# Residual loads behind the projection weights, an earlier norm order, an own constant semaphore, and a last norm without GpSimd, in an encoder block on eight cores

## The chip, the cores and the metric

The kernel runs on the 8 cores of one Trainium2 chip, two dies of four cores each. Every core computes half of one of four sequences (2048 tokens) and no core waits for another. The metric is the time on the device of the slowest core, in microseconds (us).

An execution is sometimes in a slow state: the cores of one die are granted a lower TensorE clock, and the time is longer, by 4 to 19% in the clear cases. One of the changed kernel had mean granted clocks of 0.859 to 0.862 on one die and 0.984 to 0.988 on the other, and took 1184.42 us where the fast ones took 1040.13 and 1041.25; the longest (`poke_end`) took 1240.4 instead of 1040.59.

Several chips appear. The result and the profiles of before and after come from one, called the first chip below.

## The reference, cut to what matters

```python
u = rms_norm(h, g_mix)                        # h: tokens x 1024
z = u @ w_in                                  # value, gate, pool input, two gates: 5 x 1024 columns
y_conv = conformer_conv(z[..., :c1], z[..., c1:c2], ...)   # GLU, depthwise conv, LayerNorm, swish, matmul
y_pool = multi_scale_pool(z[..., c2:c3], ...)
merged = gate_a * y_conv + gate_b * y_pool
h = h + merged @ w_o                          # output projection and residual
v = rms_norm(h, g_ffn)
h = h + (silu(v @ w_ffn_gate) * (v @ w_ffn_up)) @ w_ffn_down
return rms_norm(h, g_final)                   # the last norm
```

## The kernel before: the parts that matter

The program has a list of instructions for each engine, with waits on semaphores where data cross engines. Channels lie on the partitions and tokens along the free dimension, so the sum of squares of a norm goes through a matmul with a matrix of 1/1024, then Ln and Exp(-0.5 x) on ScalarE (ACT), and VectorE (DVE) multiplies.

The start: x comes in six pieces. Each is squared, summed and normed while TensorE (PE) already multiplies earlier pieces ("tiles" are PE work).

```python
    x_load(0)
    for (o, i_) in ((pc[:], pc_d.ap()), (invc[:], ic_d.ap()), (emask[:], em_d.ap())):
        S.dma(SP, cst, o, i_, val=48)         # three constants, ONE semaphore, all three awaited
    for p in range(NX):
        if p:
            x_load(p)                         # on the GpSimd (POOL) queue
        if p < 4:
            load_one()                        # two weight pieces, same queue
            load_one()
    ...
    s1_squares(4)                             # squares on ScalarE, sums on GpSimd
    tiles((0, 1, 2), (6,))
    s1_norm(3)
    tiles((0, 1, 2), (7,))
    tiles((3,), range(4))
    s1_squares(5)
    s1_norm(4)
    tiles((3,), range(4, KC))
    tiles((4,), range(1))
    s1_norm(5)
    ...
```

The output projection: eight weight pieces `wo0` to `wo7` come through a ring of nine slots on the GpSimd queue; the residual (x again, 4 blocks of 2 MB) comes on the SyncE (SP) queue.

```python
    for b in range(NB):
        C(6, b)
    release("co6")                            # frees the slot into which wo7 is loaded
    def x_res(b):
        S.dma(SP, h1_sem[b], h1b[b][:]..., xr_d.ap()[b])
    for b in (0, 1, 3):
        x_res(b)                              # SyncE is free: issued early
    for b in range(NB):
        C(7, b)
    release("co7")
    x_res(2)
```

The end: for the last 256 tokens, GpSimd does three of the eight multiplies of the last norm. ScalarE has multiplied those three tiles by the gain earlier, and writes 1/rms to SBUF for GpSimd.

```python
        for c in (4, 0, 5, 1, 6, 2, 3, 7) if last else range(KC):
            x = h[:, c, o:o + w_]
            if last and c in (4, 5, 6):
                tt(POOL, x, x, rs, ALU.mult)
            else:
                stt(DVE, x, x, pcc(PC_GFIN, c), psum[7][:, 0:w_], ALU.mult, ALU.mult)
        # ... then four stores of two tiles each on SyncE, and a wait for them
```

## Time and profile before

| | before |
|---|---|
| time, median (fast runs) | 1057.15 us |
| span of the slowest core (core 4) | 1052.6 us |
| PE busy | 1002.3 us (95%) |
| PE waits for the last projection weight | 4.3 us (2.1 to 5.0 on the eight cores) |
| last matmul weight load to the end of the program, core 4 | 13.7 us |

PE is busy nearly always. A change can only win where PE waits, where its clock is lowered, and at the two ends, where PE has nothing to do.

From the page of the kernel before: the busy time of each engine (PEld is PE's weight load), and the chain that ended last by engine.

```profile
PE 1002.3 (95%) x5630; PEld 489.4 (46%) x5696; DVE 449.3 (43%) x690; ACT 309.3 (29%) x504; POOL 158.5 (15%) x184
PE 86%; DMA 4%; DVE 4%; ACT 4%; issue 2%; POOL 0%; SPq 0%; ACTq 0%; POOLq 0%; DVEq 0%
```

The instructions at the line that closes the program block, kernel before, core 4 (durations in ns, then the times of the first and last start in us). A small "q" marks the engine's own sequencer.

```profile
L973 POOLq EVENT_SEMAPHORE  x2: 17/17/17, 1052.4 to 1052.5; - x2
L973 POOLq DRAIN  x1: 11366/11366/11366, 1041.0 to 1041.0; - x1
L973 SPq DRAIN  x1: 7/7/7, 1045.9 to 1045.9; - x1
```

SyncE's DRAIN comes after its wait for the last store, so all results were in memory at 1045.9 us. The program still ran until 1052.5, because GpSimd's DRAIN took 11.37 us, the first 2 us of them beside its three multiplies. It ended 9.3 us after the last of these. The chain of waits does not show this: it ends at a GpSimd multiply at 1042.3 us, and the last ten microseconds have no row.

The waits of the PE in the output projection (us in all, number, longest), and the loads there with their microseconds from issue to landing (kernel before, core 4):

```profile
PE ps L352 <- DMA wslot_60<-w_o: 4.3, 1, 4.3
```

```profile
h1b_216<-xr SPq DMA_DIRECT2D x1, 2048.0 KB, 11.4
h1b_217<-xr SPq DMA_DIRECT2D x1, 2048.0 KB, 20.5
h1b_219<-xr SPq DMA_DIRECT2D x1, 2048.0 KB, 27.0
...
wslot_61<-w_o POOLq DMA_DIRECT2D x1, 256.0 KB, 3.5
wslot_63<-w_o POOLq DMA_DIRECT2D x1, 256.0 KB, 14.8
wslot_68<-w_o POOLq DMA_DIRECT2D x1, 256.0 KB, 21.7
wslot_60<-w_o POOLq DMA_DIRECT2D x1, 256.0 KB, 23.5
```

The four weight pieces are alike. The first was issued at 490.9 us, before the residual loads of 494 us, and took 3.5 us. The others came after them and took 15 to 23.5 us; PE reached the last one 4.3 us too early.

The start: VectorE's instructions that read a piece of x, in order of time (start, us; busy, us; instruction; idle time before it and what ended that), kernel before, core 4.

```profile
13.00 2.42 DVE L373 SCALAR_TENSOR_TENSOR uT<-xb_177,pc_s,ps 128x160 bf16<-128x160 f32 x8 [3.20 <-DMA emask_s<-emask]
15.43 1.23 DVE L366 TENSOR_TENSOR sqx<-xb_178 128x1024 f32<-128x1024 f32 x1
21.92 3.22 DVE L373 SCALAR_TENSOR_TENSOR uT<-xb_178,pc_s,ps 128x256 bf16<-128x256 f32 x8 [2.61 <-ACT ps L363]
...
50.03 4.56 DVE L373 SCALAR_TENSOR_TENSOR uT<-xb_180,pc_s,ps 128x416 bf16<-128x416 f32 x8 [7.44 <-ACT ps L363]
65.55 4.82 DVE L373 SCALAR_TENSOR_TENSOR uT<-xb_181,pc_s,ps 128x448 bf16<-128x448 f32 x8 [10.96 <-ACT ps L363]
```

The rows with `uT` are the norms of pieces 0, 1, 3 and 4; the row with `sqx` squares piece 1. The first norm waits for a constant that it doesn't read (`emask`), and VectorE is idle for 7.4 and 11 us before the norms of pieces 3 and 4, waiting for ScalarE. PE pays for the latter: one of its rows at that place is

```profile
67.56 0.35 PE L352 MATMUL ps<-uT,wslot_60 128*128 128x448 bf16 x1 [0.24 <-DVE uT L373]
```

that is, matmul by matmul at the pace of VectorE.

### The profile page before, as it was taken

To read this page: it belongs to the slowest core of one execution; us is meant where nothing else is said; L and a number is where in the kernel's file an instruction comes from. 1 tells how busy PE (TensorE), PEld (TensorE's weight loads), DVE (VectorE), ACT (ScalarE), POOL (GpSimd) and SP (SyncE) were. 2 spreads that over 40 slices of the span, in tenths; PEclk is the share of its full clock that TensorE was granted. 3 is DMA by queue.
4 is the path that set the end of the run, shared out by engine and by line. 5 is a ranking of instruction groups with operands and counts; after the bars stand their busy time and mean duration, and the time that the engine had idled before them with its cause. 6 is when DMAs were issued, how large, how long until landed. Compare 5 with 4: busy or idle time off the path is not lost.

```text
span 1052.6 us, 15608 instructions; the slowest of 8 cores (1042.4 to 1052.6 us)
## 1 busy us (share of the span) xinstructions
PE 1002.3 (95%) x5630; PEld 489.4 (46%) x5696; DVE 449.3 (43%) x690; ACT 309.3 (29%) x504; POOL 158.5 (15%) x184
## 2 busy tenths in 40 slices
PE   3899999999989999999899999999999999999994
PEld 1645555555434444444344444444444444444483
DVE  4442879974279533233536521221211211343453
ACT  2643233344487611221134311111111111121121
POOL 2233022221420000000347001111000000000000
PEclk9989999999999999999999999999999999999998
DMA  9605887667253111112946445554222103312112
GB/s 219 204 0 81 167 165 160 138 160 148 59 89 61 32 31 31 31 30 59 295 177 149 102 77 95 96 92 72 41 40 34 19 1 126 115 81 81 80 81 80
DMA packets 34251, 99.90 MB, mean 95 GB/s; under 512 B 3968, under 2 KB 7168, under 8 KB 31616
## 3 DMA queue, kind: packets, MB, share of 16 engines
q0 software_dynamic: 17744, 43.00, 22.9%
q1 hardware_dynamic: 16432, 55.90, 18.3%
q8 instruction: 47, 0.77, 0.3%
q14 instruction: 28, 0.23, 0.1%
HBM read 111.93 MB, written 21.04 MB: 126 GB/s over the span
## 4 chain that ended last, share of the span: by engine, by line
PE 86%; DMA 4%; DVE 4%; ACT 4%; issue 2%; POOL 0%; SPq 0%; ACTq 0%; POOLq 0%; DVEq 0%
PE ps L352 80%; PE ps L627 5%; DMA wslot_60<-w_o 2%; DVE uT L373 1%; DMA emask_s<-emask 1%; DVE sqx L366 1%; ACT L363 1%; DMA wslot_68<-w_pool_out 1%; ACT sqx L363 0%; ACT ps L363 0%; POOL h2b_259 L366 0%; ACT zt_206 L363 0%; DVE d_2_108 L366 0%; DVE d_2_104 L366 0%; DVE d_2_100 L366 0%
## 5 line engine op out<-in xcount | busy, mean ns | idle before, releaser
L352 PE MATMUL ps<-uT,wslot_60 128*128 128x512 bf16 (+6 forms) x223 | 53.5, 360 | 9.1 <-DVE uT L373 8.3
L352 PE MATMUL ps<-mT,weff 128*128 128x512 bf16 x249 | 60.0, 385 | 0.4
L352 PE MATMUL ps<-uT,wslot_65 128*128 128x512 bf16 (+6 forms) x213 | 45.1, 357 | 0.3 <-issue 0.2
L363 ACT ACTIVATE sgf_225<-ps 128x512 f32<-128x512 f32 x30 | 17.9, 597 | 81.3 <-PE ps L352 77.6
L363 ACT ACTIVATE sgf_226<-ps 128x512 f32<-128x512 f32 x29 | 17.3, 597 | 82.3 <-PE ps L352 82.3
L352 PE MATMUL ps<-uT,wslot_61 128*128 128x416 bf16 (+6 forms) x189 | 41.2, 362 | 0.2
L363 ACT ACTIVATE sgf_227<-ps 128x512 f32<-128x512 f32 x29 | 17.3, 597 | 79.7 <-PE ps L352 79.6
L352 PEld LDWEIGHTS ps<-uT,wslot_60 128*128 128x128 bf16 x224 | 21.8, 98 | 39.1 <-issue 21.6
L352 PEld LDWEIGHTS ps<-mT,weff 128*128 128x128 bf16 x256 | 25.4, 99 | 31.3 <-issue 4.5
L352 PE MATMUL ps<-uT,wslot_62 128*128 128x416 bf16 (+6 forms) x191 | 39.5, 353 | 0.1
L352 PE MATMUL ps<-uT,wslot_64 128*128 128x416 bf16 (+6 forms) x190 | 38.5, 345 | 0.1
L352 PE MATMUL ps<-vT,wslot_64 128*128 128x512 bf16 x157 | 38.0, 382 | 0.2
L352 PE MATMUL ps<-vT,wslot_67 128*128 128x512 bf16 x156 | 37.9, 381 | 0.2
L352 PE MATMUL ps<-vT,wslot_62 128*128 128x512 bf16 x157 | 37.9, 382 | 0.2
L352 PE MATMUL ps<-vT,wslot_65 128*128 128x512 bf16 x157 | 37.6, 379 | 0.2
L352 PE MATMUL ps<-vT,wslot_66 128*128 128x512 bf16 x157 | 37.5, 380 | 0.2
L352 PE MATMUL ps<-vT,wslot_68 128*128 128x512 bf16 x157 | 37.5, 379 | 0.2
L352 PE MATMUL ps<-vT,wslot_61 128*128 128x512 bf16 x157 | 37.5, 379 | 0.2
L352 PE MATMUL ps<-vT,wslot_63 128*128 128x512 bf16 x156 | 37.4, 379 | 0.2
L366 POOL TENSOR_TENSOR h2b_259<-h2b_259,sgf_225 128x256 f32<-128x256 f32 x3 | 2.1, 717 | 214.7 <-ACT sgf_225 L363 214.7
L352 PE MATMUL ps<-uT,wslot_68 128*128 128x416 bf16 (+1 forms) x144 | 30.9, 357 | 0.0
L352 PEld LDWEIGHTS ps<-uT,wslot_65 128*128 128x128 bf16 x216 | 20.8, 98 | 21.3 <-issue 0.9
(1677 smaller groups left out, 1994.4 us busy)
## 6 DMA issues: line engine op xcount, KB each, us to landing
rep_185<-ad SPq DMA_DIRECT2D x32, 263.0 KB, 6.4
rep_186<-ad SPq DMA_DIRECT2D x32, 263.0 KB, 7.9
h2b_259<-h1d SPq DMA_DIRECT2D x2, 2048.0 KB, 9.7
h1b_216<-xr SPq DMA_DIRECT2D x1, 2048.0 KB, 11.4
h1b_217<-xr SPq DMA_DIRECT2D x1, 2048.0 KB, 20.5
h1b_219<-xr SPq DMA_DIRECT2D x1, 2048.0 KB, 27.0
h1b_218<-xr SPq DMA_DIRECT2D x1, 2048.0 KB, 18.0
h1d<-h1b_216 SPq DMA_DIRECT2D x1, 2048.0 KB, 6.3
```

Source lines behind the costliest of these rows:

```text
L352: S.op(PE, lambda e: e.matmul(out, lhsT=lhsT, rhs=rhs, start=start, stop=stop), [lhsT, rhs], [out], signal=stop if signal is None else signal)
L363: S.op(ACT, lambda e: e.activation(out=out, in_=in_, func=func, scale=scale, **kw), reads, [out])
L366: S.op(eng, lambda e: e.tensor_tensor(out=out, in0=a, in1=b, op=op), [a, b], [out])
L373: S.op(eng, lambda e: e.scalar_tensor_tensor(out=out, in0=a, scalar=s, in1=b, op0=op0, op1=op1), [a, b] + ([] if isinstance(s, float) else ...
L627: S.op(PE, lambda e, o=o, lt=lt, r_=r_, q=q, j=j: e.matmul(o, lhsT=lt, rhs=r_, start=(q == 0), stop=(q == 7), tile_position=(0, 32 * j)), ...
```

## The change

Four edits: (1) the constant `pc` gets its own semaphore; (2) the norms of pieces 3 and 4 move up in the order; (3) the first residual load goes on the GpSimd queue behind `wo7`, and the other three go on SyncE's queue after `wo7` has landed; (4) GpSimd has no part in the last norm. The diff, cut to its core:

```diff
     cst = dsem("d_const")
+    pcs = dsem("d_pc")
...
-    for (o, i_) in ((pc[:], pc_d.ap()), (invc[:], ic_d.ap()), (emask[:], em_d.ap())):
-        S.dma(SP, cst, o, i_, val=48)
+    S.dma(SP, pcs, pc[:], pc_d.ap())
+    for (o, i_) in ((invc[:], ic_d.ap()), (emask[:], em_d.ap())):
+        S.dma(SP, cst, o, i_, val=32)
...
     s1_squares(4)
-    tiles((0, 1, 2), (6,))
     s1_norm(3)
-    tiles((0, 1, 2), (7,))
-    tiles((3,), range(4))
+    tiles((0, 1, 2), (6, 7))
+    tiles((3,), range(2))
     s1_squares(5)
     s1_norm(4)
-    tiles((3,), range(4, KC))
+    tiles((3,), range(2, KC))
...
-    for b in (0, 1, 3):
-        x_res(b)
+    x_res(POOL, 0)
     for b in range(NB):
         C(7, b)
     release("co7")
-    x_res(2)
+    S.wait_prod(SP, slot_sem[whome["wo7"]])
+    for b in (1, 2, 3):
+        x_res(SP, b)
...
-            if side:
-                tt(POOL, x, x, rs, ALU.mult)
-            else:
-                stt(DVE, x, x, pcc(PC_GFIN, c), psum[7][:, 0:w_], ALU.mult, ALU.mult)
+            stt(DVE, x, x, pcc(PC_GFIN, c), psum[7][:, 0:w_], ALU.mult, ALU.mult)
+            # two tiles done: store them at once
...
-            if n == 4 and c in (4, 5, 6):
-                act(x, x, AF.Identity, scale=pcc(PC_GFIN, c))
```

More of the change, by code (lines that the diff above doesn't have):

```diff
@@ L834, in build_nc, with x_res @@
     release("co6")
-    def x_res(b):
-        S.dma(SP, h1_sem[b], h1b[b][:].rearrange("p k t -> p (k t)"), xr_d.ap()[b])
-    for b in (0, 1, 3):
-        x_res(b)
+    def x_res(eng, b):
+        S.dma(eng, h1_sem[b], h1b[b][:].rearrange("p k t -> p (k t)"), xr_d.ap()[b])
+    x_res(POOL, 0)
     for b in range(NB):
@@ L927, in build_nc, with out_norm @@
         h2_load(b)
-    def out_norm(b, o, w_, n, last=False):
+    def out_norm(b, o, w_):
         h = h2b[b % 3]
-        if last:
-            rs = sgf[0][:, 0:w_]
-            act(rs, sq1[0][:, 0:w_], AF.Exp, scale=-0.5)
-        for c in (4, 0, 5, 1, 6, 2, 3, 7) if last else range(KC):
+        for c in range(KC):
             x = h[:, c, o:o + w_]
-            side = last and c in (4, 5, 6)
-            if side:
-                tt(POOL, x, x, rs, ALU.mult)
-            else:
-                stt(DVE, x, x, pcc(PC_GFIN, c), psum[7][:, 0:w_], ALU.mult, ALU.mult)
-        if w_ < TT:
-            for c in (0, 4, 2, 6) if last else (0, 2, 4, 6):
-                S.dma(SP, out_sem, out_d.ap()[b].rearrange("p (k t) -> p k t", k=KC)[:, c:c + 2, o:o + w_],
-                      h[:, c:c + 2, o:o + w_])
+            stt(DVE, x, x, pcc(PC_GFIN, c), psum[7][:, 0:w_], ALU.mult, ALU.mult)
+            if w_ < TT and c % 2:
+                S.dma(SP, out_sem, out_d.ap()[b].rearrange("p (k t) -> p k t", k=KC)[:, c - 1:c + 1, o:o + w_],
+                      h[:, c - 1:c + 1, o:o + w_])
         if w_ == TT:
@@ L964, in build_nc @@
                 rms_stat(n - 1, pw_)
-                out_norm(pb, po, pw_, n - 1)
+                out_norm(pb, po, pw_)
                 if n == 1:
@@ L968, in build_nc @@
     rms_stat(4, 256, sq1[(KC - 1) % 3][:, 0:256])
-    out_norm(3, 256, 256, 4, True)
+    out_norm(3, 256, 256)
     S.wait_prod(SP, out_sem)
```

## The prediction

> What bounds the kernel now. The page of the slowest core (core 4, span 1052.6 us) has PE busy 1002.3 us (95%), and the chain that ended last is 86% PE. So only the PE's holes, its slow-clock spells and the two ends of the program can be won.
>
> 1. The end. In the list of instructions at the block's last line, GpSimd's DRAIN starts at 1041.0 us and takes 11.37 us; SyncE's DRAIN, which waits for the last output to land, is at 1045.9, and the end follows GpSimd's. Its last multiply ended near 1043.0, so 9.3 us of the drain come after its work. Without GpSimd work in the last norm its last instruction is a weight load near 826 us, and the drain should be over 200 us before the end. In exchange VectorE does eight multiplies instead of five: the timeline has them 0.39 us apart, from 1040.56, so the last store starts near 1043.95 instead of 1043.45. It needs 2.4 us to land. Estimate: end near 1046.6, a gain of 5.9 us.
>
> 2. Output projection. The waits of the PE show 4.3 us for its last weight piece (2.1 to 5.0 us on the eight cores). The DMA list has that piece landing 23.5 us after issue, against 3.4 to 6 us for pieces issued earlier, because three residual loads of 2 MB, issued at 494 us, share the bandwidth. The change sends two of these, and the fourth, after that piece has landed. Then it should land in 4 to 6 us and the wait is gone. The hole is followed by a half-clock spell of 3.4 us on core 4 (6.8 us on cores 1 and 2), worth 1.7 to 3.4 us.[...] The first residual, now queued behind that weight, may come some us after the first tile at 511 us, but six PSUM banks give the PE about 10 us of slack. Estimate: 6 us.
>
> 3. Norms of the x pieces. The PE waits for the norm of piece 3 from 50.9 us (1.15 us, then 0.22 us per matmul) and of piece 4 from 66.5 to 70.5 us, because ScalarE got to them late. Piece 3's norm can start 0.7 to 1 us earlier; piece 4's about 4 us earlier (61.4 instead of 65.55 us), nearly hidden. A half-clock spell at 70.1 us should vanish. Estimate: 4.5 us.
>
> 4. Own semaphore for the constants. VectorE's first norm waits until 13.0 us for the last constant; it could start at 11.85. But the next piece's squares need a DMA that lands at 15.4 us. Gain: 0.
>
> Sum: 16.4 us, nearly all on the chain. Predicted 1041.5 us, with 1035.5 to 1047.5 holding it 8 times in 10. Chances: faster by over 2% (under 1036.2 us) 0.10; within 2% 0.89; slower 0.01.
>
> What would show it: no 11 us GpSimd DRAIN at the end, under 1 us between SyncE's drain and the end; no PE wait on an output projection weight, no half clock near 525 us; piece 4's first matmuls without 0.24 us gaps; the first norm earlier but the second at the same time.
>
> What would make it wrong: the drain costs the same wherever GpSimd's work ends (then about 1047); the residuals now late enough to stall the PE[...]; the 0.81 clock in the busy output projection (core 4 shows it at 517, 539, 565 and 580 us) growing[...]; the norm of piece 4 waiting on squares that GpSimd adds (8 us).

## More of the kernel before

The experiments ran in three groups, by the record on chip 12 (each part alone), chip 13 (the two `poke` and the two `x1` runs) and chip 0 (the rest), each group beside runs of the kernel before. There the kernel before takes 1051.8 to 1053.2 us (medians) instead of 1057.15, so between chips ratios are compared, and whole times in microseconds only within a group.

## The result, and the profile after

The changed kernel takes 1042.9 us against 1057.15 (medians of 4 runs each). Two of its four runs fell in the slow state (1184.42, and 1044.55 with one die 1% longer than the other at a lower clock), the fast ones took 1041.25 and 1040.13, and a further profiled one 1040.1. The ratio of the fast runs is 0.9837, with a 95% interval of 0.9815 to 0.986: about 17.2 us. A ratio here is the mean time of one kernel's fast runs over the mean of the other's fast runs of the same rounds, so it is not quite the ratio of the medians. The gain of 1.6% is far outside the noise.

From the page of the changed kernel (its slowest core is core 7, span 1039.7 us):

```profile
PE 1005.6 (97%) x5696; PEld 489.7 (47%) x5696; DVE 450.1 (43%) x693; ACT 307.6 (30%) x500; POOL 158.0 (15%) x182
PE 91%; DMA 4%; DVE 2%; ACT 1%; issue 1%; SPq 0%; POOL 0%; DVEq 0%; ACTq 0%; POOLq 0%
```

PE's share of the chain rose from 86 to 91%: other engines' work was taken out of it. For like with like, the following lines are of core 4 again (span 1036.7 us after, 1052.6 before). First the closing line of the program:

```profile
L965 POOLq EVENT_SEMAPHORE  x2: 17/17/17, 1036.5 to 1036.6; - x2
L965 POOLq DRAIN  x1: 9847/9847/9847, 816.1 to 816.1; - x1
L965 SPq DRAIN  x1: 7/7/7, 1036.5 to 1036.5; - x1
```

GpSimd's DRAIN is not cheaper by much (9.85 us: 0.55 us until the last weight load was issued, and again 9.3 us after that), but it runs at 816 us, where nobody waits for it. The program now ends about 0.2 us after SyncE's drain.

The loads of the output projection after, core 4. There is no row left that has PE waiting for anything between 480 and 600 us.

```profile
h1b_216<-xr POOLq DMA_DIRECT2D x1, 2048.0 KB, 14.1
...
wslot_63<-w_o POOLq DMA_DIRECT2D x1, 256.0 KB, 3.6
wslot_68<-w_o POOLq DMA_DIRECT2D x1, 256.0 KB, 4.4
wslot_60<-w_o POOLq DMA_DIRECT2D x1, 256.0 KB, 4.9
```

The last weight lands in 4.9 instead of 23.5 us. The norms at the start, core 4, after:

```profile
11.62 2.42 DVE L374 SCALAR_TENSOR_TENSOR uT<-xb_177,pc_s,ps 128x160 bf16<-128x160 f32 x8 [1.97 <-ACT ps L364]
15.96 1.23 DVE L367 TENSOR_TENSOR sqx<-xb_178 128x1024 f32<-128x1024 f32 x1 [1.92 <-DMA xb_178<-xp]
22.45 3.22 DVE L374 SCALAR_TENSOR_TENSOR uT<-xb_178,pc_s,ps 128x256 bf16<-128x256 f32 x8 [2.61 <-ACT ps L364]
...
49.76 4.55 DVE L374 SCALAR_TENSOR_TENSOR uT<-xb_180,pc_s,ps 128x416 bf16<-128x416 f32 x8 [6.65 <-ACT ps L364]
61.66 4.82 DVE L374 SCALAR_TENSOR_TENSOR uT<-xb_181,pc_s,ps 128x448 bf16<-128x448 f32 x8 [7.35 <-ACT ps L364]
```

The first norm starts 1.4 us earlier and no longer waits for `emask`, but the squares of piece 1 then wait 1.92 us for that piece, and the norm of piece 1 is no earlier. The norm of piece 4 is 3.9 us earlier, and the PE row that came in single matmuls is now one unbroken row:

```profile
65.23 1.74 PE L353 MATMUL ps<-uT,wslot_60 128*128 128x448 bf16 x8
```

Where the microseconds went on core 4. I cut the span at fixed places in PE's order of instructions (the same count of weight loads in both kernels), so each row is the same work:

| stretch on core 4 | before | after | difference |
|---|---|---|---|
| start to the first value/gate weight load | 96.4 | 91.2 | -5.2 |
| to the first output projection weight load | 412.6 | 412.2 | -0.4 |
| output projection | 66.5 | 62.7 | -3.8 |
| gate and up matmuls | 306.3 | 306.0 | -0.3 |
| down matmuls | 157.0 | 157.1 | +0.1 |
| last weight load to the end | 13.7 | 7.5 | -6.2 |

The output projection is different from core to core. The same stretch in us, core 0 to core 7:

```text
before  63.4 64.7 64.9 61.2 | 66.5 65.4 63.3 61.6
after   57.6 57.6 57.6 57.6 | 62.7 62.5 62.2 62.2
```

After the change, the first die does it in exactly 57.6 us on all four cores; the second die takes 5 us more. The clock record tells why. Spells of lowered clock in the projection of core 4 (start, length in us, granted clock):

```text
before  516.9 6.7 0.8125   527.4 3.4 0.5   538.7 4.1 0.8125   565.5 6.1 0.8125
after   506.5 6.1 0.8125   518.2 10.1 0.8125   539.5 5.3 0.8125   555.5 6.7 0.8125
```

One can add it up. Before: 57.6 us of work, 4.3 of waiting, half of the 3.4 us at half clock (1.7), and 0.1875 of the 16.9 us at 0.8125 (3.2) make 66.8, measured 66.5. After: 57.6 and 0.1875 of 28.2 us (5.3) make 62.9, measured 62.7. So the change took away the wait and the half-clock spell (6.0 us, as predicted), and on this die the 0.8125 clock took 2.1 us of it back. Core 7, whose projection got no shorter (61.6 to 62.2), is now the slowest core.

In the projection the half-clock spells go with the longer waits: before the change, the five cores that waited 3.8 to 5.0 us for the last projection weight have a spell of 3.4 or 6.8 us at 0.5 there, and the three that waited 2.1 to 3.5 us have none. The spells at 0.8125 (13/16) are on all four cores of one die, but not at the same times: cores 4 and 5 have the same spells within 0.3 us, cores 6 and 7 have others (the first one of the projection after the change lasts 6.1 us on core 4 and 7.7 us on core 6). Why the spells grew from before to after is not shown; one trace of each kernel was kept from this chip.

### The profile page after: what moved, and what is told of

Its sections match the earlier page's. It is cut to its first block, busy times and chain, and to the rows that moved or that the text cites. A ratio compares the mean times of both kernels' runs of the same rounds, so it can differ in the third digit from the quotient of the medians.

```text
span 1039.7 us, 15674 instructions; the slowest of 8 cores (1026.0 to 1039.7 us)
## 1 busy us (share of the span) xinstructions
PE 1005.6 (97%) x5696; PEld 489.7 (47%) x5696; DVE 450.1 (43%) x693; ACT 307.6 (30%) x500; POOL 158.0 (15%) x182
## 4 chain that ended last, share of the span: by engine, by line
PE 91%; DMA 4%; DVE 2%; ACT 1%; issue 1%; SPq 0%; POOL 0%; DVEq 0%; ACTq 0%; POOLq 0%
PE ps L353 86%; PE ps L628 5%; DMA rep_186<-ad 2%; DMA xb_178<-xp 1%; DVE uT L374 1%; DMA ad<-aT_183 1%; DVE sqx L367 1%; DMA wslot_68<-w_pool_out 0%; ACT sqx L364 0%; ACT ps L364 0%; DVE h2b_259 L374 0%; ACT L364 0%; SPq L190 0%; ACT zt_197 L364 0%; ACT zt_203 L364 0%
## 5 line engine op out<-in xcount | busy, mean ns | idle before, releaser
L353 PE MATMUL ps<-vT,wslot_64 128*128 128x512 bf16 x160 | 38.2, 382 | 0.0
L353 PE MATMUL ps<-vT,wslot_62 128*128 128x512 bf16 x160 | 38.2, 382 | 0.0
L353 PE MATMUL ps<-vT,wslot_67 128*128 128x512 bf16 x160 | 38.1, 380 | 0.0
L353 PE MATMUL ps<-vT,wslot_66 128*128 128x512 bf16 x160 | 38.0, 380 | 0.0
L353 PE MATMUL ps<-vT,wslot_63 128*128 128x512 bf16 x160 | 37.8, 379 | 0.0
L353 PE MATMUL ps<-vT,wslot_68 128*128 128x512 bf16 x160 | 37.8, 379 | 0.0
L353 PE MATMUL ps<-vT,wslot_65 128*128 128x512 bf16 x160 | 37.8, 379 | 0.0
L353 PE MATMUL ps<-vT,wslot_61 128*128 128x512 bf16 x160 | 37.8, 379 | 0.0
L353 PE MATMUL ps<-vT,wslot_60 128*128 128x512 bf16 x128 | 30.2, 379 | 0.0
```

The lines of the kernel that those rows point to most:

```text
L353: S.op(PE, lambda e: e.matmul(out, lhsT=lhsT, rhs=rhs, start=start, stop=stop), [lhsT, rhs], [out], signal=stop if signal is None else signal)
```

## The experiments

The chips of the experiments have a useful difference: no core has a spell at 0.8125 in the clock record of any profile below (mean granted clocks of 0.987 to 0.999). There the four parts can be weighed without that disturbance. Since one part turns out to do nothing in time, `only_pc` is also the profile of "before" for the experiments.

### Each part alone

Each run is the kernel before with one of the four edits and nothing else; the edits are the four hunks of the diff above.

```diff
 only_tail      kernel before + the last norm without GpSimd
 only_residual  kernel before + the residual loads behind wo7
 only_order     kernel before + the norms of pieces 3 and 4 moved up
 only_pc        kernel before + the own semaphore of pc
```

> The kernel before with only the last norm changed (no GpSimd multiply). Theory (GpSimd's drain is fixed at some 9 to 10 us after its last instruction and was the last thing to end): the drain moves to near 816 us, the end follows SyncE's drain by under 0.3 us, and the kernel is 5.9 us faster (5.3 to 6.5), about 1051.2. Rival A (the drain costs the same wherever it stands, or stands at the end anyway): no gain, or a loss of 0.5 us from the three more VectorE multiplies. Rival B (GpSimd's multiplies were slow and held the stores): a gain of under 1 us, with the last store starting earlier than before.

> The kernel before with only the residual loads reordered. Theory (their bandwidth delayed the last projection weights): the last weight piece lands 4 to 6 us after issue instead of 21 to 23.5, the 2 to 5 us wait of the PE and the half-clock spell after it are gone, 6 us faster (4 to 7). Rival (the 13/16 clock of the busy die takes it back): the wait is gone but the stretch of the output projection is no shorter on cores 4 to 7, under 3 us faster.

> The kernel before with only the norms of the x pieces moved up. Theory: piece 4's norm starts on VectorE near 61.5 instead of 65.5 us, the PE's gaps at 66.5 to 70.5 us and the half-clock spell at 70 us go, 4.5 us faster (3.5 to 5.5). Rival (the chain is then held by the squares that GpSimd adds, or by piece 3, so that the holes only move): under 2 us.

> The kernel before with only the own semaphore for the constants. Theory (the next piece's landing near 15.5 us bounds the start anyway): the first norm starts about 1.2 us earlier, the second at the same time, 0 gain (within 0.5 us). Rival (the first norm is on the chain): 1.2 us faster.

Measured against the kernel before, in the same rounds (median 1051.79 us; one of the four runs of `only_tail` was slow and is in its median, not in its ratio):

| run | median us | ratio (95%) | gain | the stretch it should change (median of 8 cores) |
|---|---|---|---|---|
| only_tail | 1047.0 | 0.9949 (0.993 to 0.9968) | 0.51% | last weight load to end: 13.7 to 7.5 us |
| only_residual | 1044.37 | 0.9934 (0.9918 to 0.995) | 0.66% | projection: 64.8 to 57.6 us (57.6 on each core) |
| only_order | 1045.81 | 0.9947 (0.9931 to 0.9963) | 0.53% | start: 96.8 to 91.4 us |
| only_pc | 1051.91 | 1.0001 (0.9983 to 1.0019) | -0.01% | none |

All four came out as the theory said, `only_order` just above its range (0.53% is 5.6 us, 3.5 to 5.5 were expected), and the rivals fell. For the end, these are the rows of the closing line of `only_tail`:

```profile
L963 POOLq DRAIN  x1: 9847/9847/9847, 822.0 to 822.0; - x1
L963 SPq DRAIN  x1: 7/7/7, 1042.7 to 1042.7; - x1
```

For the residual loads, PE's wait for a projection weight (4.9 us on the slowest core of `only_pc`) is absent in `only_residual`, and so is the half-clock spell (core by core, between 519 and 526 us) that all eight cores of `only_tail` and `only_pc` have. Without the 0.8125 clock on this chip, the gain is the full 7 us of the stretch, where the first chip's second die kept 3.8 us or less.

For the own semaphore, the rows of VectorE in `only_pc` (core 6) show the gain appear and vanish within 5 us:

```profile
10.54 2.42 DVE L374 SCALAR_TENSOR_TENSOR uT<-xb,pc_s,ps 128x160 bf16<-128x160 f32 x8 [1.97 <-ACT ps L364]
14.86 1.23 DVE L367 TENSOR_TENSOR sqx<-xb 128x1024 f32<-128x1024 f32 x1 [1.90 <-DMA xb<-xp]
```

### The four parts together, without the 0.8125 clock

The changed kernel, unedited:

```diff
 after_again    the changed kernel as it is
```

> The changed kernel as it is, on the chip of the other runs of this call. If the four parts add up (0.51, 0.66, 0.53 and 0.0% when alone), it is 1.7% faster than the kernel before, ratio 0.983 (0.981 to 0.985).

Measured: 1034.31 us (5 runs, 1033.56 to 1035.26), ratio 0.9823 (0.9807 to 0.9839). The parts alone sum to 0.51 + 0.66 + 0.53 - 0.01 = 1.69%, the whole gives 1.77%. The two agree within the noise (0.16% on the whole alone), as independent gains at three different places of one PE-bound chain should. The first chip's ratio was 0.9837; the projection of all cores takes 57.6 us here.

### Is it GpSimd's drain, or GpSimd's slow multiplies?

`only_tail` alone can't quite tell whether the drain or the three multiplies and the store order made the end long. So a GpSimd instruction that does nearly nothing, and whose result nobody reads, was put back into the changed kernel, at two places.

```diff
 poke_end
     out_norm(3, 256, 256)
+    tt(POOL, sq1[1][:, 0:8], h2b[0][:, 7, 256:264], h2b[0][:, 7, 256:264], ALU.mult)

 poke_c5   (in the loop over the last eight output tiles)
+            if n == 4 and c == 5:
+                tt(POOL, sgf[1][:, 0:8], x[:, 0:8], x[:, 0:8], ALU.mult)
```

> The changed kernel with one GpSimd multiply of 8 columns, whose result nobody uses, after the last multiply of the last norm. Theory (a drain that lasts a fixed 9.3 us beyond the last GpSimd work): GpSimd's DRAIN ends some 9.3 us after that multiply, near 6.7 us after SyncE's drain, and the kernel is 6 to 7 us slower than the changed one, with the stores where they were. Rival (the three slow multiplies, or the store order, made the old end long): under 0.5 us slower.

> The changed kernel with the same small GpSimd multiply, but at the sixth of the eight output tiles of the last part, some 11 us before SyncE's drain. Theory (fixed 9.3 us after the last GpSimd work): the DRAIN ends 1 to 2 us before SyncE's, no change of time (within 1 us). Rival (any GpSimd work late in the program costs its drain in full at the end): 6 us slower.

The rows of the closing line, `poke_end` first, then `poke_c5` (the slowest core of each):

```profile
L966 POOLq DRAIN  x1: 9544/9544/9544, 1029.3 to 1029.3; - x1
L966 SPq DRAIN  x1: 7/7/7, 1031.3 to 1031.3; - x1
```

```profile
L967 POOLq DRAIN  x1: 9546/9546/9546, 1018.8 to 1018.8; - x1
L967 SPq DRAIN  x1: 7/7/7, 1031.5 to 1031.5; - x1
```

With one multiply of 8 columns at the very end, SyncE's drain is where it should be, but GpSimd's lasts until 1029.3 + 9.54 = 1038.8 us, and the program with it (span 1039.0). On all eight cores the stretch from the last weight load to the end is 15.0 us, twice the 7.5 of the changed kernel. The time was 1040.59 us in its one fast run (the other slow at 1240.4), 7.0 us above the fast runs of `poke_c5` (below) on the same chip; the changed kernel's own 1034.31 is from another chip.

With the same multiply at the sixth of the last eight output tiles, 12.5 us before SyncE's drain, GpSimd's drain ends at 1028.3 us, 3.2 us before SyncE's (1 to 2 us were expected), and the stretch is 7.5 us again: 1033.27 and 1033.9 us in its fast runs, about the time of the changed kernel. So the cost is shown. In all 14 kept traces and on every core, GpSimd's DRAIN ends 9.3 us after the end of GpSimd's last instruction, be that a multiply (as before and in the two `poke` runs) or the issue of a weight load (as in the changed kernel). In these runs it costs time only where the last instruction ends less than 9.3 us before the last result has landed.

### Queue or order?

The change also moved the first residual load to another queue. This run undoes that move and keeps the order.

```diff
 resid_sp
-    x_res(POOL, 0)
...
-    for b in (1, 2, 3):
+    for b in range(NB):
         x_res(SP, b)
```

> The changed kernel with the first residual load on SyncE's queue too, behind the last projection weight. Theory (what matters is the order behind the weights, not the queue): the weight lands in about 4 us as in the changed kernel, the residual lands some us later (near 520 us), the PE's six PSUM banks nearly hide it; same time within 2 us. Rival (the GpSimd queue for the first residual is what does it): the wait of 2 to 5 us for the last weight comes back.

Measured: 1036.63 us (median of four, one of them slow; the fast ones 1032.96 to 1037.53), ratio 0.9831 (0.9806 to 0.9857), not distinguishable from 0.9823. The projection takes 57.6 to 58.1 us on the eight cores. On the slowest core the first residual tile is added at 516.6 us, and PE waited 0.3 us for a PSUM bank (a part of the memory that matmuls write to) there. So the order behind the weights is what matters; the GpSimd queue for the first block buys at most 0.5 us of the projection here, less than the times can tell apart (0.26%, or 2.7 us).

What the two queues moved in the kernel before, between 485 and 545 us (core 4; packets, MB, share of the 16 engines' time):

```profile
q1 hardware_dynamic: 720, 10.49, 51.0%
q0 software_dynamic: 720, 1.31, 13.6%
```

A packet of the residual loads' queue has 10.49 MB / 720 = 14.6 KB, one of the weights' queue 1.8 KB. The weights landed in 15 to 23.5 us beside the residual loads, and in 3.6 to 4.9 us ahead of them (core 4, after). Whether the small packets made the delay this long is not shown: no run here changed the packet size.

### Two locks on one door: why the own semaphore gained nothing

In the profile after, the first norm is early and then piece 1 of x is late. So piece 1 was issued before the first two weight pieces, once with the own semaphore of the changed kernel, once with the shared one of before.

```diff
 x1_first: changed kernel, x1_shared: changed kernel with the constants on one semaphore; in both
+    x_load(1)
     for p in range(NX):
-        if p:
+        if p > 1:
             x_load(p)
```

> The changed kernel with x piece 1 issued before the first two weight pieces. Theory (with the own semaphore the only thing that holds the second piece's squares is the landing of x piece 1): it lands near 13 instead of 15.5 us, the squares start near 14.1, right after the first norm, and the second norm starts 1.4 us earlier (0.8 to 2): 1 to 2 us faster than the changed kernel. Rival (the first weights, now later, hold the PE): no gain.

> The same early x piece 1, but with the constants on one shared semaphore as in the kernel before. Theory (two things hold the same start, and neither alone helps): VectorE's first norm waits for the last constant until near 13 us and ends near 15.4, so the squares start no earlier than in the changed kernel: 0 gain (within 0.5 us), 1 to 1.5 us slower than with the own semaphore.

Measured: `x1_first` 1030.18 us, ratio 0.9793 (0.9776 to 0.9809); `x1_shared` 1033.97 us, ratio 0.983 (0.9815 to 0.9845). The start of the second norm, median of the eight cores, is at 22.7 us in the changed kernel (`after_again`), 19.9 in `x1_first` and 23.1 in `x1_shared`. VectorE's rows, `x1_first` (core 4), then `x1_shared` (core 7):

```profile
11.42 2.42 DVE L374 SCALAR_TENSOR_TENSOR uT<-xb,pc_s,ps 128x160 bf16<-128x160 f32 x8 [1.97 <-ACT ps L364]
13.76 1.22 DVE L367 TENSOR_TENSOR sqx<-xb 128x1024 f32<-128x1024 f32 x1
```

```profile
14.72 2.42 DVE L373 SCALAR_TENSOR_TENSOR uT<-xb,pc_s,ps 128x160 bf16<-128x160 f32 x8 [6.56 <-DMA emask_s<-emask]
17.06 1.22 DVE L366 TENSOR_TENSOR sqx<-xb 128x1024 f32<-128x1024 f32 x1
```

In `x1_first` the squares of piece 1 follow the first norm without a gap. In `x1_shared` that piece is there too (it landed 9.3 us after issue), but VectorE is still held by the semaphore of a constant. The own semaphore alone gains nothing (`only_pc`, on the kernel before, 1.0001), and the early load with the shared semaphore gains nothing either (`x1_shared` 0.983, the changed kernel 0.9823); together they gain 0.3%. The 0.9823 is from another chip; on that of the `x1` runs, `poke_c5`, which is the changed kernel with one harmless multiply, took 1033.6 us (mean of its fast runs), which says the same. The direction was as expected and the sizes were not: the gain over the changed kernel is 3.1 us (1 to 2 expected, by the ratios 0.9823 and 0.9793), and the two differ by 3.8 us (1 to 1.5 expected). I had not counted that the early piece 1 delays the constants' landing: on the slowest core of each, `emask` took 12.1 us in `x1_shared` and 10.5 in `after_again`. PE waits 3.9 us for its first weight in `x1_first`, which costs nothing, since it would otherwise wait for the second norm.

### A better order for piece 3

In the changed kernel PE still goes matmul by matmul at piece 3, from 50 to 54 us. ScalarE does four squares of 0.87 us for piece 4 before the Ln and Exp of piece 3. This run puts the norm first, and gives piece 4's norm two tiles more time.

```diff
 norm3_first
-    s1_squares(4)
     s1_norm(3)
+    s1_squares(4)
     tiles((0, 1, 2), (6, 7))
     tiles((3,), range(2))
     s1_squares(5)
+    tiles((3,), range(2, 4))
     s1_norm(4)
-    tiles((3,), range(2, KC))
+    tiles((3,), range(4, KC))

 combined: norm3_first and x1_first together
```

> The changed kernel with the norm of piece 3 ahead of the squares of piece 4, and piece 4's norm two tiles later. Theory (ScalarE's order alone holds piece 3's norm, 4 squares of 0.87 us): piece 3's norm starts near 46.5 instead of 49.3 us, the PE's gaps from 50 to 54 us shrink, 2 to 4 us faster than the changed kernel. Rival (GpSimd's adds for piece 4, now later, become the wait): the gain is lost at piece 4, under 1 us.

> Norm of piece 3 first and x piece 1 first, together on the changed kernel. Theory (both shorten the same chain at different places): the gains add, 4 to 6 us faster than the changed kernel, ratio to the kernel before near 0.978 (0.976 to 0.981). Rival: later DMA landings of x pieces 3 to 5 (up to 46 us) hold the earlier norms, and less than 3 us is left.

The row of piece 3's norm in `norm3_first` (core 3):

```profile
46.67 4.56 DVE L374 SCALAR_TENSOR_TENSOR uT<-xb,pc_s,ps 128x416 bf16<-128x416 f32 x8 [3.67 <-ACT ps L364]
```

It starts at 46.8 us in the median of the cores, where `after_again` has 50.0. The time is 1030.96 us, ratio 0.9791 (0.9775 to 0.9808), or 3.3 us less than the changed kernel. GpSimd's adds for piece 4 did not become the wait: piece 4's norm is 2.7 us earlier too (59.6 against 62.3). `combined` takes 1028.24 us (1027.15 to 1029.9), ratio 0.9765 (0.9747 to 0.9783): 6.1 us less than the changed kernel and 2.35% less than the kernel before. It was the fastest kernel, and its results were correct. The start, up to the first value/gate weight load, is 96.8 us in `only_pc`, 91.9 in `after_again`, 89.0 in `norm3_first`, 89.7 in `x1_first` and 86.8 in `combined`.

## Why the prediction was right, point by point

The measured median of 1042.9 us lies inside the range of 1035.5 to 1047.5, 1.4 us above the central value of 1041.5; the mean of the fast runs, 1040.5, is 1.0 us below it.

- **The end (5.9 us predicted).** Right in mechanism and size. The stretch went from 13.7 to 7.5 us, 6.2 us, on the first chip and in `only_tail`. `poke_end` and `poke_c5` show that the fixed time after GpSimd's last work is the cause.
- **The output projection (6 us predicted).** The wait and the half-clock spell went, and on core 4 they were 4.3 and 1.7 us, 6.0 in all. The stretch fell by 3.6 to 7.3 us on the first die, but only by 3.8 us or less on the second, where the 0.8125 clock grew, from 16.9 to 28.2 us in this stretch of core 4. The prediction named that risk and did not charge for it: this is the term that was mis-sized on the first chip; whether the vanished wait made the spells grow is not shown. In `only_residual`, without those spells, the stretch fell by 7.2 us.
- **The norms (4.5 us predicted).** Right. The norm of piece 4 was foretold for 61.4 us and started at 61.66 on core 4; the start became 5.2 us shorter there, 5.4 in `only_order`. The half-clock spell at 70 us went.
- **The constants (0 predicted).** Right, and `x1_first` and `x1_shared` show the reason given, the landing of piece 1.
- **Sum.** 16.4 us predicted; 15.9 measured on core 4 (1052.6 to 1036.7), 17.2 between the means of the fast runs, 14.25 between the medians, of which the later one includes two slow runs. The slowest core, which sets the time, is another one after the change, and its share of the 0.8125 spells differs from run to run, so an agreement within 1 us is partly luck.

## What to carry to other kernels

Look at what stands between the last landing and the end of the program: an engine that has work late can have a closing cost that no chain of waits shows (9.3 us for GpSimd here), and moving its last instruction some 10 us up is as good as making it fast (in `poke_c5` the stretch was 7.5 us, as without that instruction). Issue loads in the order of need, not as soon as an issuing engine is free: three early loads of data needed later cost the PE here a hole of 2.1 to 5.0 us and, on most cores, a half-clock spell of 3.4 or 6.8 us. When one of two waits that end within 2 us of each other is taken away, expect nothing until the other goes too, and try both before giving up on either.

## The closing DRAINs, the clock and the loads, as measured

- Of the DRAINs that close the program's own block, SyncE's took 7 ns, but GpSimd's took 9.85 us with a weight load's issue still to finish, 9.54 us with one multiply of 8 columns, and 11.37 us with three multiplies of 0.7 us each: 9.3 us beyond its last instruction each time.
- In the fast profiled runs here all eight cores ran dense matmuls for over 450 us of gate, up and down work at a granted clock of 1.0, with one spell of 5.9 us on cores 6 and 7 of the first chip; the spells at 0.8125 lasted 3.7 to 10.1 us, nearly all between 306 and 328 us and in and just after the output projection, on one die of the first chip and on none of the experiments' chips. (In the slow run of `poke_end` the four cores of one die had a mean granted clock of 0.814 to 0.818. No trace of a slow run was kept.)
- 256 KB of projection weights took 3.5 us when issued ahead of the residual loads, and up to 23.5 us beside three loads of 2 MB; the packets there were 1.8 KB against 14.6 KB.
